# The norm's factor leaves the first half's input projection and enters behind it

## The chip, the cores and the metric

The kernel runs on one core of a Trainium2 chip. The metric is the device time of one execution in microseconds; of several runs the median counts. Engines are named as in the profile: PE is TensorE, DVE is VectorE, ACT is ScalarE, POOL is GpSimd, SP is SyncE, which issues all DMA transfers here.

## The reference

One decoder layer on x of 2048 positions by 1024 features, all in float32. Cut to what the change touches:

```python
h = rmsnorm(x, norm1_g)              # h = x * f * g, f = rsqrt(mean(x*x) + eps) for each position
proj = h @ w_in
p_q, p_k, p_v, p_g, p_a, c_b, c_c, c_h = split(proj)
q, k, v = p_q * 64**-0.5, p_k, p_v   # 4 heads, 64 wide for q and k, 128 for v
log_a = log_sigmoid(p_a @ w_gate_up + b_gate) / 16
o = gla_chunked(q, k, v, log_a)      # gated linear attention with a carried state
o = rmsnorm(o, gla_norm_g) * silu(p_g)
u = c_c * c_h
o_conv = c_b * causal_depthwise_conv(u, conv_w)   # three taps along positions
x = x + concat(o, o_conv) @ w_out
h2 = rmsnorm(x, norm2_g)
x = x + (silu(h2 @ w_ffn_gate) * (h2 @ w_ffn_up)) @ w_ffn_down
out = rmsnorm(x, norm_f_g)
```

The factor f is one number for each position, so it can be taken out of the projection: proj is f times (x * g) @ w_in. The attention is linear in v; its output is normalised by head, so a factor of q drops out but for the small eps, and k and v enter as a product.

## The kernel before, in words

Positions are handled in four blocks of 512 (`PB`), two to a half. A tile has 128 partitions and 512 columns; features lie on partitions, positions on columns. The halves go one after the other through the input projection (`in_proj`), then both through the output projection and the feed-forward part.

The input projection of a half has twelve units. A unit makes a block of two output row tiles by two position blocks from four weight quarters (A11, A12, A21, A22; 128 by 512 each) and the input operands. Units 2 to 11 (`unit`) use seven products of sums and differences instead of eight (S1 to S4 of weights on POOL, T1 to T4 of inputs on POOL); each product is four contraction steps. Unit 0 (`build_first`) and unit 1 (`plain_unit`) use eight plain products, since the differences of inputs are made meanwhile (`differences`). Units 0 to 3 give k, q and v, units 4 and 5 the swish gate (`silu`), units 6 to 11 the convolution: 6 and 9 give c_c, 7 and 10 c_h, 8 and 11 c_b.

Every float32 operand is split in two (`split`): ACT copies it to a rounded high part (L153), DVE subtracts that from it for the low part (L154). A step is then three matmuls: high by high, high by low, low by high (L366 to L368 in a unit; L297 to L299 in unit 0). The weight quarters are split so too (`weight_quarter`), into a pool of four buffers (`wqp`), so splits run at most four quarters ahead. Operands (`op`) have 28 buffers; the x rows of the norm share them.

In the beginning `first_loads` loads, in this order: x rows of block 0 (positions on partitions, for the squares), the weights of unit 0 and the input tiles `h` of block 0 (from `xt`, which is x with features on partitions), x rows of block 1, the input tiles of block 1. `row_squares` sums the squares on ACT, `rows_rstd` makes the factor (Ln and Exp on ACT, a Newton step on DVE), spreads it and transposes it on PE into a PSUM bank (`rb_ps`), and `scaled` (L490) multiplies an input tile by gain and factor in place. Then the tile is split and multiplied.

Work beside the units is written as generators in a list (`background`); `tick`, called after each product, runs one step of the first of them. In the first half these are, in turn, `gate_weights`, a pause, `row_stats` of blocks 2 and 3, `gate` (the forget gate: Abs, Exp, Ln on ACT, scans on DVE), `h1_ahead` (the second half's operands) and, from unit 6 on, `gla_half`. A scheduler sets each engine's final order from the program and its dependences; each engine then runs its instructions strictly in that order.

## Time and profile before

| | |
|---|---|
| median of 3 runs | 2110.91 us |
| lowest and highest | 2108.93 and 2113.38 us |
| profiled execution, span from first to last instruction | 2109.1 us |
| profiled execution, its own time | not listed apart from the span |
| PE, DVE, ACT, POOL busy | 2033.1, 1418.4, 1014.1, 972.4 us |
| mean granted clock of PE | 0.992 |
| HBM traffic | 219 GB/s over the span |

A row of the timeline gives the start in us from the span's start, the duration, engine, line, operation, output<-inputs, partitions x elements, and in brackets how long the engine stood idle before and what ended that. A row of waits gives the waiting instruction, what it waited for, the total, how often, and the longest. A row of a group gives its count, then busy time and the mean of one in ns, then the idle time before. A row of windows gives a stretch, its length, and the busy time of PE, weight loads, DVE, ACT and POOL (with counts), the granted clock, the DMA share and GB/s.

### The profile page before, as it was taken

What the parts mean: (1) busy time and instruction counts of PE and PEld (TensorE: products, weight loads), DVE (VectorE), ACT (ScalarE), POOL (GpSimd) and SP (SyncE); (2) the same over time, 40 slices, a digit from 0 to 9 for tenths busy, and PEclk for the clock granted to TensorE, in tenths of its full rate; (3) what the DMA queues carried; (4) which work ended last, traced back from release to release, by engine and by line L of the source; (5) the groups of instructions that cost most, each with busy time, mean ns of one, the idle gap of its engine ahead of it and who ended that gap; (6) DMA issues with size and microseconds to landing.
All of it is one profiled execution on the core that took longest, in us unless ns stands there. A gap on an engine that the chain in (4) does not pass through costs nothing.

```text
span 2109.1 us, 26874 instructions
## 1 busy us (share of the span) xinstructions
PE 2033.1 (96%) x9133; PEld 1648.9 (78%) x9133; DVE 1418.4 (67%) x1983; ACT 1014.1 (48%) x1997; POOL 972.4 (46%) x703
## 2 busy tenths in 40 slices
PE   5999999999999999999999999999999989999996
PEld 4778888877888878788888878787888868877775
DVE  7669786549753786788786665554766666665564
ACT  5555455656542356445545443333554554543344
POOL 3436322222102464564464348764645544436774
PEclk9999999999999999999999999999999999999998
DMA  7349485425586872656545687697454535587763
GB/s 277 126 158 318 139 329 164 148 83 164 201 284 235 325 249 100 241 198 221 217 172 220 243 327 272 235 338 296 158 207 179 206 134 190 183 344 281 269 269 110
DMA packets 189241, 464.43 MB, mean 220 GB/s; under 512 B 19824, under 2 KB 65072, under 8 KB 179504
## 3 DMA queue, kind: packets, MB, share of 16 engines
q1 hardware_dynamic: 189104, 462.72, 60.4%
q8 instruction: 72, 1.18, 0.2%
q14 instruction: 65, 0.53, 0.1%
HBM read 297.49 MB, written 165.15 MB: 219 GB/s over the span
## 4 chain that ended last, share of the span: by engine, by line
PE 70%; DVE 8%; DMA 7%; ACT 3%; issue 3%; POOL 2%; SPq 0%; DVEq 0%; ACTq 0%; POOLq 0%
PE mm L366 21%; PE mm L368 21%; PE mm L367 21%; DVE wq L154 2%; DMA op<-shT 1%; DVE so L154 1%; PE mm L794 1%; DVE h L490 1%; PE mm L795 1%; PE mm L797 1%; DVE op L154 1%; DMA sx<-y 1%; ACT wq L153 1%; PE o_ps L718 1%; DMA shT<-so 1%
## 5 line engine op out<-in xcount | busy, mean ns | idle before, releaser
L366 PE MATMUL mm<-op,wq 128*128 128x512 f32 x2499 | 981.3, 395 | 23.8 <-DVE c L390 7.8
L368 PE MATMUL mm<-op,wq 128*128 128x512 f32 x2499 | 966.1, 392 | 12.6 <-DVE wq L154 11.9
L367 PE MATMUL mm<-op,wq 128*128 128x512 f32 x2499 | 976.0, 391 | 0.0
L154 DVE TENSOR_TENSOR wq<-raw,wq 128x512 fp32r<-128x512 f32 (+2 forms) x626 | 527.3, 849 | 329.9 <-ACT wq L153 324.3
L153 ACT ACTIVATE wq<-raw 128x512 fp32r<-128x512 f32 (+2 forms) x626 | 363.6, 587 | 555.8 <-PE mm L368 402.4
L366 PEld LDWEIGHTS mm<-op,wq 128*128 128x128 f32 x2499 | 470.8, 188 | 137.6 <-ACT wq L153 12.3
L368 PEld LDWEIGHTS mm<-op,wq 128*128 128x128 f32 x2499 | 470.5, 188 | 123.5 <-DVE wq L154 24.8
L367 PEld LDWEIGHTS mm<-op,wq 128*128 128x128 f32 x2499 | 471.2, 189 | 96.7 <-issue 1.0
L351 POOL TENSOR_TENSOR raw<-s,raw 128x512 f32<-128x512 f32 (+2 forms) x97 | 127.5, 1314 | 422.2 <-DVE wq L154 402.0
L390 DVE TENSOR_TENSOR c<-mm,c 128x512 f32<-128x512 f32 x267 | 183.0, 686 | 95.7 <-PE mm L368 93.0
L349 POOL TENSOR_TENSOR s<-raw 128x512 f32<-128x512 f32 (+2 forms) x97 | 130.2, 1343 | 216.2 <-DMA raw<-in_wffn_dram 88.8
L356 POOL TENSOR_TENSOR raw<-raw 128x512 f32<-128x512 f32 (+2 forms) x97 | 126.7, 1306 | 135.3 <-DVE wq L154 128.1
L386 ACT ACTIVATE c<-mm 128x512 f32<-128x512 f32 x267 | 154.7, 585 | 38.0 <-PE mm L368 36.8
L776 POOL TENSOR_TENSOR ssx<-ssx,q 128x512 f32<-128x512 f32 x52 | 76.5, 1483 | 156.0 <-ACT q L775 155.8
L350 POOL TENSOR_TENSOR raw<-raw 128x512 f32<-128x512 f32 (+2 forms) x97 | 135.1, 1393 | 4.1
L965 POOL TENSOR_TENSOR y<-c,y 128x512 f32<-128x512 f32 x66 | 98.7, 1499 | 49.0 <-DVE c L390 46.6
L154 DVE TENSOR_TENSOR so<-t,so 128x512 fp32r<-128x512 f32 x100 | 91.2, 918 | 25.9 <-ACT so L153 25.4
L153 ACT ACTIVATE wq<-s 128x512 fp32r<-128x512 f32 (+2 forms) x97 | 56.9, 586 | 93.5 <-PE mm L368 83.3
L794 PE MATMUL mm<-op,wq 128*128 128x512 f32 x256 | 100.9, 395 | 0.0
L795 PE MATMUL mm<-op,wq 128*128 128x512 f32 x256 | 99.8, 390 | 0.0
L154 DVE TENSOR_TENSOR wq<-s,wq 128x512 fp32r<-128x512 f32 (+2 forms) x97 | 84.1, 867 | 15.6 <-ACT wq L153 15.0
L153 ACT ACTIVATE so<-t 128x512 fp32r<-128x512 f32 x100 | 62.5, 627 | 41.8 <-DMA sa_T<-so 16.1
(177 smaller groups left out, 1885.0 us busy)
## 6 DMA issues: line engine op xcount, KB each, us to landing
raw<-in_wffn_dram SPq DMA_DIRECT2D x44, 1024.0 KB, 5.7
sa_T<-so SPq DMA_DIRECT2D x88, 512.0 KB, 5.3
op<-sa_T SPq DMA_DIRECT2D x88, 512.0 KB, 9.2
sa_B<-so SPq DMA_DIRECT2D x69, 512.0 KB, 3.4
op<-sa_B SPq DMA_DIRECT2D x69, 512.0 KB, 9.0
raw<-in_win_dram SPq DMA_DIRECT2D x23, 1024.0 KB, 5.5
raw<-in_wdown_dram SPq DMA_DIRECT2D x24, 768.0 KB, 6.2
sx<-y SPq DMA_DIRECT2D x48, 256.0 KB, 3.2
```

The source lines that it names most:

```text
L153: last_hi[:] = [act.activation(hi, src, AF.Copy)]
L154: return dve.tensor_tensor(lo, src, hi.bitcast(F32), ALU.subtract)
L349: pool.tensor_tensor(s1, a21, a22, ALU.add)
L350: pool.tensor_tensor(a21, a11, a21, ALU.subtract)
L351: pool.tensor_tensor(a11, s1, a11, ALU.subtract)
L356: pool.tensor_tensor(a12, a12, a11, ALU.subtract)
L366: pe.matmul(o[:], wh, xh, start=first and k == 0, stop=False, skip_group_check=True)
L367: pe.matmul(o[:], wh, xl, start=False, stop=False, skip_group_check=True)
L368: return pe.matmul(o[:], wl, xh, start=False, stop=k == n - 1, skip_group_check=True)
L386: act.activation(t[:], o[:], AF.Copy)
L390: dve.tensor_tensor(t[:], o[:], t[:], ALU.add)
L794: pe.matmul(o[e, j][:], wh, m[:, 0, :], start=k == 0, stop=False)
```

## The change

The first half's unit 0 takes input times gain only. ACT's copy to the high part and DVE's subtraction carry the gain, and POOL multiplies the tile by it in place for the later differences. The x rows, their squares and the factor move behind: the rows are loaded after all input tiles and after unit 1's weights, and the squares are a background task (`first_stats`). The factor then enters in the forget gate's input, the swish gate and c_c (c_c by its square; c_h is not multiplied), the convolution's result (once more), the value's copy in the attention (by its square, with positions on partitions) and, as a scale, the normalisation of the attention's output. Twelve matmuls of ones by ones stand at the start. The second half is as it was.

```diff
...
@@ -270,25 +270,37 @@
             put("B22", k, b22)
             yield
 
-    def build_first(quad, w):
+    def build_first(h, raw):
 
 
         ops = {b: [] for _, b in PRODUCTS}
-        h, o = {}, {}
+        o, out, w = {}, [], {}
         quarters = ("A11", "A12"), ("A21", "A22")
-        los = []
+        order = []
+
+        def turn(n, i):
+            with ExitStack() as stack:
+                if order:
+                    stack.enter_context(tc.issue_after(order[-1].ins))
+                w[n] = weight_quarter(raw[:, i, :])
+            order.append(last_hi[0])
+
         for j in range(2):
             for r in range(2):
                 o[r, j] = bank()
             for k in range(KD):
-                with ExitStack() as stack:
-                    if len(los) > 1:
-                        stack.enter_context(tc.issue_after(los[-2].ins))
-                    h[k, j] = quad(k, j)
+                g = col(C_G1 + k)
+                if j == 0 and k in (0, 3, 4):
+                    turn(*{0: ("A11", 0), 3: ("A12", 1), 4: ("A22", 2)}[k])
                 x = opp.tile([P, 2, PB], F32R, name="op", tag="op")
-                los.append(split(h[k, j][:], x[:, 0, :], x[:, 1, :]))
-                if j == 0 and k >= PT:
-                    row_squares(1, k - PT)
+                with tc.issue_after(order[-1].ins):
+                    order.append(act.activation(x[:, 0, :], h[k, j][:], AF.Copy, scale=g))
+                if (k, j) == (0, 0):
+                    turn("A21", 3)
+                dve.scalar_tensor_tensor(
+                    x[:, 1, :], h[k, j][:], g, x[:, 0, :].bitcast(F32), ALU.mult, ALU.subtract
+                )
+                pool.tensor_scalar(h[k, j][:], h[k, j][:], g, 1.0, ALU.mult, ALU.mult)
...
-            if j == 0:
-                rbs[1] = rows_rstd(squares[1])
-
+            out += [(r, j, settled(o[r, j], True), False) for r in range(2)]
         def differences(wanted):
             for n, y, a, b in (
                 ("T1", (0, 0), (0, 1), (0, 0)), ("T2", (0, 0), (4, 1), (0, 0)),
...
@@ -446,9 +455,26 @@
         dve.tensor_tensor(ssq[:, :, 0], ssq[:, :, 0], ssq[:, :, 1], ALU.add)
         rbs[b] = rows_rstd(ssq)
 
-    def rows_rstd(ssq):
-
-        v, l, y0 = [mtiny.tile([P, PT], F32, name=n, tag=n) for n in ("msq", "rl", "ry")]
+    def first_stats():
+        yield from pause(1)
+        for b in range(2):
+            for t in range(PT):
+                row_squares(b, t)
+                if t % 2:
+                    yield
+        yield from pause(3)
+        for b in range(2):
+            f, f2 = [mtiny.tile([P, PT], F32, name=n, tag=f"{n}{b}", bufs=1) for n in ("f", "ff")]
+            factors[b] = tiny.tile([P, PB], F32, name="rb", tag="rb")
+            act.activation(factors[b][:], rows_rstd(squares[b], f)[:], AF.Copy)
+            dve.tensor_tensor(f2[:], f[:], f[:], ALU.mult)
+            positions[b] = f, f2
+            yield
+
+    def rows_rstd(ssq, v=None):
+
+        l, y0 = [mtiny.tile([P, PT], F32, name=n, tag=n) for n in ("rl", "ry")]
+        v = v or mtiny.tile([P, PT], F32, name="msq", tag="msq")
...
-    rbs, raws, first_weights, last_load, rows, squares = {}, {}, {}, [], {}, {}
+    rbs, raws, positions, rows, squares, factors, factors2 = {}, {}, {}, {}, {}, {}, {}
 
     def row_squares(b, t):
         act.activation(rows[b, t], rows[b, t], AF.Square, accum_out=squares[b][:, t, 0:1])
@@ -466,6 +492,14 @@
     def first_loads():
 
         raw = rawp.tile([P, 4, PB], F32, name="raw", tag="raw")
+        for j in range(2):
+            for k in range(KD):
+                if j == 0 and k % 4 == 0:
+                    for i in ((0, 3), (1, 2))[k // 4]:
+                        raw_loads.append(load(raw[:, i, :], win[0][:, i, :]))
+                h = raws[k, j] = bt("h") if len(raws) > 4 else tt("h")
+                load(h[:], xt[j, :, k, :])
+        second = raw_weights(win[1])
         for b in range(2):
             squares[b] = mtiny.tile([P, PT, 2], F32, name="ssq", tag="ssq")
             for t in range(PT):
@@ -473,18 +507,7 @@
...
-            for k in range(KD):
-                if b == 0 and k % 4 == 0:
-                    for i in ((0, 3), (1, 2))[k // 4]:
-                        raw_loads.append(load(raw[:, i, :], win[0][:, i, :]))
-                h = bt("h") if b else tt("h")
-                raws[b, k] = h
-                last_load[:] = [load(h[:], xt[b, :, k, :])]
-        for t in range(PT):
-            row_squares(0, t)
-        rbs[0] = rows_rstd(squares[0])
-        for n, i in (("A11", 0), ("A21", 3), ("A12", 1), ("A22", 2)):
-            first_weights[n] = weight_quarter(raw[:, i, :])
+        return raw, second
 
...
-    def build_h():
-
-
-        def quad(k, j):
-            return scaled(col(C_G1 + k), rbs[j], raws[j, k])
-
-        return build_first(quad, first_weights)
+    def factored(c, in_psum, f):
+
+        s = tt("n") if in_psum else c
+        (dve if in_psum else pool).tensor_tensor(s[:], c[:], f[:], ALU.mult)
+        return s
 
     def h1_ahead():
 
@@ -560,7 +581,12 @@
                         stop=n == "B22" and k == 3 and e == 1, skip_group_check=True,
                     )
         a_sb = bt("a_sb")
-        act.activation(a_sb[:], a[:], AF.Copy)
+        if half:
+            act.activation(a_sb[:], a[:], AF.Copy)
+        else:
+            for j in range(2):
+                r = slice(32 * j, 32 * j + 32)
+                dve.tensor_tensor(a_sb[r, :], a[r, :], factors[j][r, :], ALU.mult)
         yield
         for j in range(2):
             small = decays[2 * half + j] = [
...
+        def values(u):
+            f = factors2 if u in (6, 9) else factors
+            for r, j, c, p in next(units):
+                if half == 0 and u in (4, 5, 6, 9):
+                    c, p = factored(c, p, f[j]), False
+                yield r, j, c, p
+
         def units():
             for u in range(12):
-                with ExitStack() as stack:
-                    if half == 0 and u == 1:
-                        stack.enter_context(tc.issue_after(last_load[0].ins))
-                    if half or u > 1:
-                        us = unit(win[u], ops)
-                    else:
-                        us = plain_unit(win[u], ops) if u else first
+                if half or u > 1:
+                    us = unit(win[u], ops)
+                else:
+                    us = plain_unit(second, ops) if u else first
                 if half == 0 and u == 1:
                     del ops["B12"]
                     differences(("T4",))
@@ -611,16 +641,21 @@
         units = units()
         if half == 0:
             differences(("T1", "T2", "T3"))
-        for dst, i0 in ((s_kq, 0), (s_kq, 2), (s_v, 0), (s_v, 2)):
-            for r, j, c, p in next(units):
+        for u, (dst, i0) in enumerate(((s_kq, 0), (s_kq, 2), (s_v, 0), (s_v, 2))):
+            for r, j, c, p in values(u):
                 store(dst[2 * half + j][i0 + r][:], settled(c, p)[:])
         for i0 in (0, 2):
-            for r, j, c, p in next(units):
+            for r, j, c, p in values(4 + i0 // 2):
                 store(s_g[2 * half + j][i0 + r][:], silu(c, p)[:])
         background.append(gla_half(half))
+        if half == 0:
+            for j in range(2):
+                factors2[j] = tiny.tile([P, PB], F32, name=f"rr{j}", tag=f"ssx{j}", bufs=1)
+                act.activation(factors2[j][:], factors[j][:], AF.Square)
         for i0 in (0, 2):
-            cc = {(r, j): settled(c, p) for r, j, c, p in next(units)}
-            ch = {(r, j): c for r, j, c, _ in next(units)}
+            u = 6 + 3 * (i0 // 2)
+            cc = {(r, j): settled(c, p) for r, j, c, p in values(u)}
+            ch = {(r, j): c for r, j, c, _ in values(u + 1)}
...
@@ -635,9 +670,11 @@
                         dve.scalar_tensor_tensor(
                             y[:], s[:, n : n + PB], col(C_CW + 4 * n + i), y[:], ALU.mult, ALU.add
                         )
+                    if half == 0:
+                        pool.tensor_tensor(y[:], y[:], factors[j][:], ALU.mult)
                 if half == 0:
                     act.activation(halo[:, i, :], left, AF.Copy)
-            for r, j, c, _ in next(units):
+            for r, j, c, _ in values(u + 2):
                 y = cc[r, j]
                 dve.tensor_tensor(y[:], c[:], y[:], ALU.mult)
                 hi = tp.tile([P, PB], F32R, name="hi", tag="t")
@@ -702,7 +739,10 @@
         for h in range(HEADS):
             pe.transpose(v_ps[:, h, :], v[:, h, :], ident[:])
         act.activation(kt[:, 0:2, :], kt_ps[:], AF.Copy)
-        act.activation(v[:], v_ps[:], AF.Copy)
+        if b in positions:
+            act.activation(v[:], v_ps[:], AF.Copy, scale=positions[b][1][:, t : t + 1])
+        else:
+            act.activation(v[:], v_ps[:], AF.Copy)
         if b or t:
             em = decays[b][0]
             for h in range(HEADS):
@@ -739,9 +779,12 @@
         ssq, l, y0 = [mtiny.tile([P, HEADS], F32, name=n, tag=n) for n in ("hsq", "hl", "hy")]
         sq = mtiny.tile([P, P], F32, name="sq", tag="rep")
         for h in range(HEADS):
-            act.activation(sq[:], o[:, h, :], AF.Square, accum_out=ssq[:, h : h + 1])
+            f = positions[b][0][:, t : t + 1] if b in positions else 1.0
+            act.activation(sq[:], o[:, h, :], AF.Square, scale=f, accum_out=ssq[:, h : h + 1])
         dve.tensor_scalar(ssq[:], ssq[:], 1.0 / P, EPS, ALU.mult, ALU.add)
         rsqrt(ssq[:], ssq[:], l[:], y0[:])
+        if b in positions:
+            dve.tensor_scalar(ssq[:], ssq[:], f, None, ALU.mult)
         osb = bt("osb", (P, HEADS, P))
         rs = ssq[:].rearrange("p (h c) -> p h c", c=1).to_broadcast([P, HEADS, P])
         dve.tensor_tensor(osb[:], o[:], rs, ALU.mult)
@@ -1046,19 +1089,22 @@
             scale(j, rbs[j])
 
 
+    warm = bank("warm")
+    for _ in range(12):
+        pe.matmul(warm[:, 0:P], ones[:], ones[:], start=True, stop=True)
     act.preload_act_table_set("natural_log_exp_and_others")
-    first_loads()
+    raw, second = first_loads()
     for i in range(4):
         load(wgu_sb[16 * i : 16 * i + 16, :], wgu[0:16, :])
-    ops, first, differences = build_h()
+    ops, first, differences = build_first(raws, raw)
     hurry.append(True)
     background.extend(
         [
-            gate_weights(), pause(9), row_stats(2), row_stats(3), gate(0, ops), unhurried(),
+            gate_weights(), first_stats(), pause(2), row_stats(2), row_stats(3), gate(0, ops), unhurried(),
             h1_ahead(),
         ]
     )
-    in_proj(0, ops, first, differences)
+    in_proj(0, ops, first, second, differences)
     drain_background(lambda: len(background) < 2)
     ops = load_pairs(s_h1)
     background.append(gate(1, ops))
```

The places where the order of ACT changes, each before and then of the changed kernel. First, ACT from its first instruction after the table load; `xr` is an x row, `wq` a weight quarter's split, `op` an input operand's high part, `rl` and `ry` the root.

```order
L464 ACTIVATE xr,ssq<-xr 128x1024 x4
L153 ACTIVATE wq<-raw 128x512
L158 ACTIVATE rl<-msq 128x4
L153 ACTIVATE wq<-raw 128x512
L159 ACTIVATE ry<-rl 128x4
L153 ACTIVATE wq<-raw 128x512 x2
L153 ACTIVATE op<-h 128x512 x3
L464 ACTIVATE xr,ssq<-xr 128x1024
```

```order
L153 ACTIVATE wq<-raw 128x512
L297 ACTIVATE op<-h,sml 128x512
L153 ACTIVATE wq<-raw 128x512
L297 ACTIVATE op<-h,sml 128x512 x2
L153 ACTIVATE wq<-raw 128x512
L297 ACTIVATE op<-h,sml 128x512
L153 ACTIVATE wq<-raw 128x512
L297 ACTIVATE op<-h,sml 128x512 x12
```

The four squares and the root leave the place ahead of the first operands; weight quarters and the sixteen operands come first.

Second, ACT where unit 1's first two weight quarters are split (the last `wq` rows of each piece; `op<-h` are the differences' high parts, `wa_sb` the gate's weights, `xn` rows of block 2).

```order
L153 ACTIVATE op<-h 128x512 x2
L153 ACTIVATE wa_sb<-wa 128x4x16 x3
L153 ACTIVATE op<-h 128x512 x2
L444 ACTIVATE xn,ssq<-xn 128x512
L153 ACTIVATE op<-h 128x512
L444 ACTIVATE xn,ssq<-xn 128x512
L415 ACTIVATE c_807<-mm 128x512
L153 ACTIVATE op<-h 128x512
L153 ACTIVATE wq<-raw 128x512 x2
```

```order
L490 ACTIVATE xr,ssq<-xr 128x1024
L153 ACTIVATE op<-h 128x512
L424 ACTIVATE c_637<-mm 128x512
L490 ACTIVATE xr,ssq<-xr 128x1024
L424 ACTIVATE c_639<-mm 128x512
L490 ACTIVATE xr,ssq<-xr 128x1024
L158 ACTIVATE rl<-f 128x4
L153 ACTIVATE op<-h 128x512
L490 ACTIVATE xr,ssq<-xr 128x1024
L153 ACTIVATE wq<-raw 128x512
L153 ACTIVATE op<-h 128x512
L153 ACTIVATE wq<-raw 128x512
```

Squares of x rows of block 1, which stood among unit 0's operands, now stand here; the last of the eight is directly ahead of unit 1's first quarter.

Third, ACT in units 4 and 5, where Silu of the swish gate (L422, now L431) meets the forget gate's Exp and Ln (L590 and L592; now L608, L609, L616).

```order
L590 ACTIVATE em<-g_1489 128x4
L422 ACT_TABLE_LOAD
L422 ACTIVATE c_1437<-c_1437 128x512
L153 ACTIVATE hi<-t_1625 128x512
L422 ACTIVATE c_1505<-c_1505 128x512
L592 ACT_TABLE_LOAD
L592 ACTIVATE el<-g_1490 128x4
L153 ACTIVATE wq<-raw 128x512 x2
L422 ACT_TABLE_LOAD
L422 ACTIVATE c_1473<-c_1473 128x512
L153 ACTIVATE hi<-t_1625 128x512
L153 ACTIVATE wq<-raw 128x512
```

```order
L609 ACT_TABLE_LOAD
L609 ACTIVATE g_1521<-g_1521,ones 128x512
L431 ACT_TABLE_LOAD
L431 ACTIVATE c_1435<-c_1435 128x512
L616 ACT_TABLE_LOAD
L616 ACTIVATE em<-g_1487 128x4
L608 ACTIVATE g_1552<-g_1552 128x512
L153 ACTIVATE wq<-raw 128x512
L609 ACT_TABLE_LOAD
L609 ACTIVATE g_1552<-g_1552,ones 128x512
L431 ACT_TABLE_LOAD
L431 ACTIVATE c_1470<-c_1470 128x512
```

The two kinds, which need different tables, now alternate; up to the attention's own table load there are 14 loads in ACT's order where there were 4. Each Silu of a value that is not in PSUM now follows a multiply on POOL.

7 lines of the change are left out of this document (3 added, 4 removed).

## The prediction

> **What bounds the kernel now.** I read the page's share of busy time first, then TensorE's waits over the first 400 us, then the timeline of the start.
>
> ```profile
> PE 2033.1 (96%) x9133; PEld 1648.9 (78%) x9133; DVE 1418.4 (67%) x1983; ACT 1014.1 (48%) x1997; POOL 972.4 (46%) x703
> ```
>
> TensorE is busy for 96% of the span, so a microsecond counts only where TensorE stands still or runs slowly. The waits of TensorE, 0 to 400 us (total, times, longest):
>
> ```profile
> PE rb_ps L458 <- DVE rep L457: 14.3, 2, 14.1
> PE mm L368 <- DVE wq L154: 4.2, 2, 2.1
> PE mm L297 <- ACT op L153: 3.8, 2, 2.3
> ```
>
> The largest is at the very start, and these three, but for half of the second, fall in the first 66 us. The timeline (start, duration, engine, line, instruction) shows why:
>
> ```profile
> 1.24 1.84 SPq L145 DMA_DIRECT2D xr<-in_x_dram  x4
> ...
> 4.88 1.06 ACT L464 ACTIVATE xr<-xr 128x1024 f32<-128x1024 f32 x1 [2.80 <-DMA xr<-in_x_dram]
> ...
> 6.83 1.06 ACT L464 ACTIVATE xr<-xr 128x1024 f32<-128x1024 f32 x1 [0.80 <-DMA xr<-in_x_dram]
> ...
> 14.07 1.45 PE L458 MATMUL rb_ps<-ident,rep 128*128 128x128 f32 x4 [14.07 <-DVE rep L457]
> ...
> 17.16 1.13 ACT L153 ACTIVATE op<-h 128x512 fp32r<-128x512 f32 x2
> ...
> 17.83 1.22 PE L297 MATMUL mm<-op,wq 128*128 128x512 f32 x2 [2.30 <-ACT op L153]
> ...
> 19.85 0.63 PE L298 MATMUL mm<-op,wq 128*128 128x512 f32 x1
> ...
> 20.28 0.63 PE L299 MATMUL mm<-op,wq 128*128 128x512 f32 x1
> ...
> 23.79 0.39 PE L298 MATMUL mm<-op,wq 128*128 128x512 f32 x1
> ...
> 24.02 0.39 PE L299 MATMUL mm<-op,wq 128*128 128x512 f32 x1
> ```
>
> The first transfers are rows of x (1.24), only for the norm. Their squares (4.88 on), the root and the transposes (14.07) precede the first projection matmul at 17.83. Its matmuls follow each other in 0.43 us (19.85 to 20.28) until 23.79 and in 0.23 us after: 5.96 us at half the rate, a loss of 3 us. It comes back later:
>
> ```profile
> 65.16 0.79 PE L368 MATMUL mm<-op,wq 128*128 128x512 f32 x1 [2.06 <-DVE wq L154]
> ...
> 71.24 0.40 PE L367 MATMUL mm<-op,wq 128*128 128x512 f32 x1
> ```
>
> After short waits TensorE is slow for another 6.1 us (65.16 to 71.24). The landmark by which I compare the kernels is the third product of the third unit, where the seven-product units get under way. ScalarE copies the first two products out here:
>
> ```profile
> 81.54 0.58 ACT L386 ACTIVATE c<-mm 128x512 f32<-128x512 f32 x1
> ...
> 84.32 0.58 ACT L386 ACTIVATE c<-mm 128x512 f32<-128x512 f32 x1
> ```
>
> So that product starts at 84.3. A unit of eight products is 96 matmuls, 21.8 us at 0.227; two of them and two products more are 21.8 + 21.8 + 5.4 = 49 us. Some 35 us of the 84.3 are start, waits and slow clock: that is all the change can win. Later TensorE is the bound, and what the front wins is kept unless later stages lose it.
>
> **The change, part by part.** *First matmul.* No x row stands ahead now; two quarter-megabyte weights and then the first input tile do. In the rows above 512 KB arrived at 4.88 and the next at 6.83, so 768 KB arrives at about 5.8. Split to matmul took 0.67 us (17.16 to 17.83): 6.5 us instead of 17.83. The 12 warm-up matmuls have no row; the nearest are the transposes at 14.07, of that shape, 4 in 1.45 us. Twelve take 4.4 us (at most 12 x 0.43 = 5.2), from about 1.1, when their operand is set: they end before 6.5 and cost nothing. If they bring full rate, unit 0 ends at 6.5 + 21.8 = 28.3; if not, at 31.3.
>
> *Second unit.* ScalarE's order puts all eight row squares ahead of this unit's first split, and the x rows are now last in the queue. Ahead of and with the eighth row 10.5 MB are moved. The windows (busy us of each engine, clock, DMA share, GB/s) give the rate:
>
> ```profile
> 0.00:10.00 10.00, 0.00 (x0) 0.00 (x0) 2.10 (x7) 5.14 (x8) 1.11 (x7) 1.00 0.74 259
> 10.00:20.00 10.00, 3.52 (x9) 2.13 (x10) 7.19 (x18) 4.90 (x11) 0.00 (x0) 1.00 1.02 357
> 20.00:30.00 10.00, 10.00 (x39) 8.07 (x38) 8.15 (x18) 7.28 (x16) 0.00 (x0) 1.00 0.99 361
> ...
> 40.00:50.00 10.00, 8.61 (x36) 6.55 (x37) 10.00 (x12) 7.97 (x19) 8.49 (x6) 1.00 0.53 185
> 50.00:60.00 10.00, 10.00 (x46) 8.28 (x45) 9.97 (x11) 4.59 (x14) 7.46 (x6) 1.00 0.45 157
> 60.00:70.00 10.00, 6.84 (x19) 4.80 (x18) 9.93 (x14) 10.00 (x26) 5.33 (x4) 0.72 0.53 182
> ...
> 80.00:90.00 10.00, 10.00 (x46) 8.28 (x45) 2.86 (x5) 3.70 (x7) 1.29 (x1) 1.00 0.21 65
> ```
>
> 259, 357 and 361 GB/s over 10 us each are 9.8 MB by 30; the eighth row lands at about 32. Its square (1.06) and the split (0.6) put the unit's start at 34: 3 to 6 us after unit 0, a new wait. One long enough for the slow clock, as before 65.16, so 3 us more. TensorE is through two units and two products at 34 + 21.8 + 5.4 + 3 = 64 (61 without the clock).
>
> By the Trainium skill (TensorE: Matmul & The Clock Gate, Part 1) the gate opens after one busy window of about 3.4 us. The rows show 5.96 and 6.1; by the page the loss would be 1.7, not 3, and the time 1.3 us less.
>
> *SyncE.* The input tiles now take the buffers that the gate weights and the later x rows had free, so their loads wait in SyncE's queue for GpSimd's differences, and stores and the fourth unit's weights stand behind them. ScalarE splits the gate weights ahead of the second half of unit 1's weights:
>
> ```profile
> wa<-in_wa_dram SPq DMA_DIRECT2D x1, 128.0 KB, 4.6
> ```
>
> The seventh difference comes at about 7 + 16 x 1.4 + 7 x 1.58 = 40 (prices below), the landing 4.6 later: 45. TensorE needs those weights at 34 + 10.9 = 45, or 48 if slow. It just fits; each microsecond later is one lost, up to the 66 below, which VectorE sets anyhow.
>
> *VectorE and GpSimd up to the landmark.* Can they feed it?
>
> ```profile
> 1.40 0.41 POOL L80 TENSOR_SCALAR_AFFINE_SELECT mask<-mask 128x256 f32<-128x256 f32 x1
> ...
> 18.09 0.69 DVE L154 TENSOR_TENSOR op<-h,op 128x512 fp32r<-128x512 f32 x1
> ...
> 49.35 6.98 DVE L154 TENSOR_TENSOR op<-h,op 128x512 fp32r<-128x512 f32 x6
> L310 POOL TENSOR_TENSOR h<-h 128x512 f32<-128x512 f32 x16 | 24.9, 1579 | 38.5 <-DVE h L490 33.2 <-DVE op L154 5.3
> L490 DVE SCALAR_TENSOR_TENSOR h<-h,sml,rb_ps 128x512 f32<-128x512 f32 x32 | 23.4, 738 | 1.0 <-PE rb_ps L458 1.0
> ```
>
> The scaling by norm and gain (L490, one operand in PSUM) goes: 16 x 0.74 = 12 us of VectorE, since the gain is now inside the low-half subtraction. That subtraction reads two SBUF tensors; such a one took 0.69 alone (18.09) and 1.16 each while GpSimd ran (six in 6.98). In order, 63 VectorE instructions precede and include the low half of the third product's weights. In 40 to 70 us, with GpSimd busy, 37 took 29.9 us, 0.81 each: 51 us from about 5, plus some 6 us in which they wait for the x rows (27 to 33): 62. GpSimd gets 16 gain multiplies without a row here. The bounds are twice the 128x256 select, 0.8, and L310's 1.58; I take 1.4, near the two-operand ones. With 16 differences at 1.58 and three weight sums that is 22 + 25 + 4 = 52 us from 7: 59. The last differences go GpSimd, ScalarE, VectorE in turn ahead of that product's weights, which adds some 4: 66, the latest of the three, is my value; bounds 61 (TensorE alone) and 69. The gain at the landmark is 84.3 - 66 = **18.3 us** (15 to 23).
>
> *Moved work.* The factor's eight transposes stood in the idle front and now stand among the third and fourth unit's products:
>
> ```profile
> 32.09 0.47 PE L458 MATMUL rb_ps<-ident,rep 128*128 128x128 f32 x2 [0.21 <-DVE rep L457]
> ```
>
> 0.24 each, 1.9 us, and 1 us of waits for their operand: **+3** (2 to 4). The copies and squares of the factor on ScalarE, and the row statistics, find the slack that 80 to 90 shows (VectorE 2.86 of 10, ScalarE 3.70); four more full ScalarE instructions would be 2.4 us if it were gone.
>
> *Gate and Silu.* The gate comes a few ticks later and its exponentials now alternate with the Silus: 14 table loads instead of 4 up to the GLA's.
>
> ```profile
> 150.89 1.28 ACT L592 ACT_TABLE_LOAD   x1
> 152.18 0.21 ACT L592 ACTIVATE el<-g 128x4 f32<-128x4 f32 x1
> 152.30 1.13 ACT L153 ACTIVATE wq<-raw 128x512 fp32r<-128x512 f32 x2
> 153.45 1.28 ACT L422 ACT_TABLE_LOAD   x1
> 154.74 0.63 ACT L422 ACTIVATE c<-c 128x512 f32<-128x512 f32 x1
> 155.28 0.62 ACT L153 ACTIVATE hi<-t 128x512 fp32r<-128x512 f32 x1
> ```
>
> A load takes 1.29 (150.89 to 152.18), a four-element instruction 0.12, a full one 0.54. From the first to the last split of the sixth unit stand 38: 9 loads, 5 small, 24 full: 11.6 + 0.6 + 13 = 25 us. TensorE needs 84 x 0.227 = 19.1 us for the unit, and the four weight buffers let splits run three products (8.2 us) ahead. The fifth split comes about 2 us late. Waits for GpSimd's multiplies can add to it. The stage already loses time:
>
> ```profile
> 151.46 0.50 PE L368 MATMUL mm<-op,wq 128*128 128x512 f32 x1 [2.11 <-DVE wq L154]
> ```
>
> I take **+2** (-1 to +9).
>
> By the Trainium skill (ScalarE: Activation LUTs, What ACT_TABLE_LOAD costs) a switch costs 2.66 us with its drain; the rows show no drain, and the sum goes by 1.29. What a drain would do is a rival below.
>
> *Factors.* Twenty GpSimd multiplies at 1.4 to 1.58 (12 on values, 8 on the convolution) are 30 us spread over some 150, beside TensorE's work; they slow VectorE's two-operand instructions. **+1** (0 to 4). The scale on the value copy is free, the extra four-element multiply in each of eight tiles is a microsecond in all, off TensorE's path. If that cover fails, it is the second rival.
>
> Sum: -18.3 + 3 + 2 + 1 = **-12.3 us**: span 2109.1 to 2096.8. The median lies 1.8 us above the profiled span, so **2098.5**.
>
> **Rivals.** *The chains keep up.* The landmark is set by TensorE: at 61 with the x-row wait, at 28.3 + 21.8 + 5.4 = 55.5 without. Gain 23 to 29 less 2: **2084 to 2090**. For it: VectorE has 12 us less. Against: it read 10.00, 9.97 and 9.93 of 10 in 40 to 70, and GpSimd now starts at 7 instead of 33. Chance 0.13.
>
> *VectorE stays the bound.* If all 46 large instructions cost 1.16 and 17 small 0.3, with the 6 us of waiting, VectorE needs 5 + 59 + 6 = 70 and the landmark is 72: gain 12, less 6: **2105**. For it: the six in 6.98. Chance 0.16.
>
> *Slower: ScalarE's queue blocks in the Silu stage.* Six Silus now wait for a GpSimd multiply, and weight splits queue behind them. In GpSimd's queue the multiplies stand among weight sums that wait for VectorE:
>
> ```profile
> L351 POOL TENSOR_TENSOR raw<-s,raw 128x512 f32<-128x512 f32 x13 | 19.5, 1497 | 84.1 <-DVE wq L154 84.1
> ```
>
> 84.1 us over 13, 6.5 each. If four of the six meet such a wait, 26 us less the lead of 8.2 is 18, with the loads 20: 18.3 - 3 - 20 - 1 = -5.7, **2116.5**. It turns slower from a loss of 18.5 us there. Against: three multiplies have a product's time or more before their Silu. Chance 0.08.
>
> *A drain at each table switch*, as long as the load: 9 x 1.29 more, a stall of 14 instead of 2: **2110.5**, no change. Against: 150.89 starts where the Silu before it ends. It is the page's rule above. Chance 0.03.
>
> **How the numbers follow.** The forecast (2092 to 2104) has 0.58, the rivals 0.13, 0.16, 0.08, 0.03, and 0.02 is left for a shift of later waits that eats it. 0.2% (4.2 us) is about what a measurement of this kernel tells from no change. Faster: 0.58 + 0.13 + 0.12 of the second = 0.83. Same: 0.04 + 0.03 + 0.02 = 0.09. Slower: 0.08. The range 2086 to 2109 takes in the bounds (23 with no later loss; 15 less 4, 6 and 4), most of the first two rivals, and leaves out 0.18.
>
> **What would show it.** Right: first projection matmul at 6 to 8 us; TensorE idle between the first two units until the eighth square, near 33; the copy after the second product near 66; short waits for weights where table loads alternate. Wrong: a landmark after 75, waits of over 3 us on Silu-stage splits, or TensorE's waits grown after 300 us.

## The result and the profile after

| | before | after |
|---|---|---|
| median | 2110.86 us (2108.93 to 2113.38) | 2131.68 us (2126.77 to 2134.14) |
| ratio to before, 95% interval | | 1.0098, 1.0085 to 1.0111 |
| profiled span, clock | 2109.1 us | 2129.5 us, 0.986 |

The change makes the kernel 1% slower, some 21 us, where the prediction had 12 us of gain and a range of 2086 to 2109. (A ratio, here and below, is the one on record; it can stand up to 0.1% beside the quotient of the medians shown.) The page's busy shares of the changed kernel:

```profile
PE 2048.7 (96%) x9157; PEld 1657.4 (78%) x9157; DVE 1431.3 (67%) x1983; ACT 1032.2 (48%) x2008; POOL 1025.6 (48%) x739
```

TensorE is busy for 15.6 of the 20.4 us by which the span has grown: 4.6 are the warm-up matmuls below, and the granted clock is lower behind the waits. The timeline of TensorE at the start:

```profile
1.12 4.59 PE L1094 MATMUL warm<-ones 128*128 128x128 f32 x24 [1.12 <-DVE ones L77]
7.73 1.32 PE L309 MATMUL mm<-op,wq 128*128 128x512 f32 x2 [2.02 <-ACT op L297]
...
31.16 0.39 PE L311 MATMUL mm<-op,wq 128*128 128x512 f32 x1
...
35.79 0.80 PE L375 MATMUL mm<-op,wq 128*128 128x512 f32 x1 [4.24 <-ACT wq L153]
...
74.42 0.79 PE L375 MATMUL mm<-op,wq 128*128 128x512 f32 x1 [8.69 <-ACT c L395]
```

The first projection starts at 7.73 instead of 17.83, and unit 0 is over at 31.5. Then 4.24 us of waiting between the units, as forecast, and at 65.7 a stop of 8.69 us that was not: the third product of unit 2 waits until ScalarE has copied the first one out of PSUM. ScalarE's timeline there (the squares of the late rows `xn` at L453, the copies at L395):

```profile
66.89 0.62 ACT L453 ACTIVATE xn<-xn 128x512 f32<-128x512 f32 x1
...
68.02 0.62 ACT L453 ACTIVATE xn<-xn 128x512 f32<-128x512 f32 x1
...
73.79 0.58 ACT L395 ACTIVATE c<-mm 128x512 f32<-128x512 f32 x1
...
75.67 0.58 ACT L395 ACTIVATE c<-mm 128x512 f32<-128x512 f32 x1
```

The copies, at 81.54 and 84.32 before, come 7.8 and 8.7 us sooner: half of the 18.3 that the sum took. By 257 us everything is gone and more. ScalarE's timeline has the last copy of unit 9, before and after in one fence each:

```profile
240.29 0.60 ACT L386 ACTIVATE c<-mm 128x512 f32<-128x512 f32 x1 [2.04 <-PE mm L368]
```

```profile
256.73 0.60 ACT L395 ACTIVATE c<-mm 128x512 f32<-128x512 f32 x1 [2.08 <-PE mm L377]
```

That is 16.4 us late; from 417 us on it is 19 to 20, and that stays. So 25 us are lost between 76 and 257 us and 3 behind it. The chain that ended last shows the first place, unit 5 (start, duration, engine, line):

```profile
145.87 1.28 ACT L431
147.81 1.28 ACT L616
150.37 1.28 ACT L609
152.41 1.28 ACT L431
154.35 1.28 ACT L618
```

Each of these is a table load: the forget gate's Ln (L609) and its two small Exp (L616, L618) alternate with Silu (L431), and weight splits stand behind them. The waits of TensorE (total, times, longest), 100 to 200 us and then the largest of 200 to 400 us:

```profile
PE mm L377 <- DVE wq L154: 3.2, 2, 2.9
PE mm L375 <- ACT c L395: 1.9, 1, 1.9
PE mm L375 <- ACT wq L153: 1.8, 1, 1.8
...
PE mm L377 <- DVE wq L154: 6.4, 9, 1.7
```

Before, these waits were 3.0 us from 100 to 200, and none is listed from 200 to 400. The windows (busy us of each engine with its instructions, clock, DMA share, GB/s), before and then after, show how VectorE falls behind in the later units:

```profile
100.00:120.00 20.00, 20.00 (x92) 16.30 (x91) 6.55 (x13) 5.62 (x10) 4.18 (x4) 1.00 0.25 93
120.00:140.00 20.00, 20.00 (x76) 13.61 (x76) 12.76 (x29) 12.96 (x26) 1.30 (x1) 1.00 0.27 92
140.00:160.00 20.00, 17.58 (x74) 13.28 (x72) 20.00 (x27) 12.92 (x23) 13.00 (x8) 1.00 0.79 270
```

```profile
100.00:120.00 20.00, 20.00 (x91) 16.38 (x90) 9.04 (x16) 6.02 (x11) 5.16 (x4) 1.00 0.29 105
120.00:140.00 20.00, 20.00 (x77) 13.30 (x75) 9.74 (x15) 8.27 (x13) 2.60 (x2) 1.00 0.15 53
140.00:160.00 20.00, 16.05 (x57) 12.01 (x57) 17.75 (x26) 19.28 (x28) 9.94 (x7) 0.87 0.43 145
...
220.00:240.00 20.00, 15.85 (x64) 11.25 (x62) 20.00 (x23) 8.36 (x17) 13.76 (x8) 1.00 0.47 149
```

From 100 to 140 VectorE is busy for 18.8 of 40 us, no more than before (19.3), though TensorE is 8 to 12 us further on: its background work has not come along. Behind that it is busiest (20.00 of 20 from 160 to 180 and 220 to 240), when the gate's scans, the second half's h and the convolution all want it.

### The profile page after: what moved, and what is told of

Same layout as the page of the kernel before. It is cut to its first block, busy times and chain, and to the rows that moved or that the text cites. A ratio compares the mean times of both kernels' runs of the same rounds, so it can differ in the third digit from the quotient of the medians.

```text
span 2129.5 us, 27006 instructions
## 1 busy us (share of the span) xinstructions
PE 2048.7 (96%) x9157; PEld 1657.4 (78%) x9157; DVE 1431.3 (67%) x1983; ACT 1032.2 (48%) x2008; POOL 1025.6 (48%) x739
## 4 chain that ended last, share of the span: by engine, by line
PE 72%; DVE 10%; DMA 6%; ACT 5%; issue 3%; POOL 3%; SPq 0%; DVEq 0%; POOLq 0%; ACTq 0%
PE mm L375 21%; PE mm L377 21%; PE mm L376 21%; DVE wq L154 2%; PE mm L837 2%; PE mm L838 2%; PE mm L840 2%; DVE h L513 1%; DVE so L154 1%; DMA raw<-in_wffn_dram 1%; DVE op L154 1%; DMA raw<-in_wdown_dram 1%; DMA h<-in_xt_dram 1%; ACT wq L153 1%; PE a_ps L579 1%
## 5 line engine op out<-in xcount | busy, mean ns | idle before, releaser
L395 ACT ACTIVATE c<-mm 128x512 f32<-128x512 f32 x267 | 154.9, 585 | 33.6 <-PE mm L377 32.0
L153 ACT ACTIVATE wq<-s 128x512 fp32r<-128x512 f32 (+2 forms) x97 | 56.7, 585 | 92.3 <-PE mm L377 85.3
```

The costliest lines, as they stand in the source:

```text
L153: last_hi[:] = [act.activation(hi, src, AF.Copy)]
L395: act.activation(t[:], o[:], AF.Copy)
```

## The experiments

Each ran beside the kernel before on its own chip, but the groups of experiments were on different chips, so runs of different groups are compared by their ratios. "Copies" are the starts of the first two copies in unit 2 and of the last in unit 9, in the profiled execution (before 81.5, 84.3, 240.3; after 73.8, 75.7, 256.7).

| run | edit, to which kernel | median us | ratio, 95% interval | copies |
|---|---|---|---|---|
| e1 | after, no factor multiplies | 2130.06 | 1.0083 (1.0066 to 1.0100) | 73.2, 75.1, 252.8 |
| e2 | after, gate ahead of the late rows' statistics | 2109.68 | 0.9987 (0.9975 to 0.9999) | 65.1, 69.3, 233.9 |
| e3 | after, late rows and gate 7 steps later | 2141.43 | 1.0137 (1.0118 to 1.0155) | 74.0, 75.9, 265.8 |
| e4 | before, gate 4 steps later | 2135.25 | 1.0108 (1.0090 to 1.0126) | 81.0, 83.8, 261.4 |
| e5 | before, with the multiplies (by ones) | 2123.49 | 1.0045 (1.0029 to 1.0061) | 79.0, 81.8, 252.2 |
| e6 | e2 without multiplies | 2097.26 | 0.9921 (0.9904 to 0.9938) | 65.4, 69.5, 225.2 |
| e8 | after, no pauses ahead of the gate, gate first | 2118.02 | 1.0023 (1.0013 to 1.0032) | 71.6, 82.2, 243.0 |
| e9 | before, 4 steps' pause behind the gate | 2112.39 | 1.0004 (0.9992 to 1.0017) | 78.7, 81.5, 237.5 |
| e10 | after, copy for Silu everywhere | 2124.89 | 1.0060 (1.0037 to 1.0083) | 74.0, 75.9, 253.8 |
| e11 | e2, second half's h spread out | 2108.69 | 0.9990 (0.9979 to 1.0001) | 65.4, 69.6, 234.8 |
| e12 | e2, all multiplies on VectorE | 2107.33 | 0.9979 (0.9967 to 0.9992) | 63.3, 68.9, 232.1 |
| e13 | e1, copy for Silu everywhere | 2112.60 | 1.0002 (0.9990 to 1.0015) | 74.5, 76.4, 247.5 |
| e14 | e2, convolution's multiplies on VectorE | 2107.27 | 0.9974 (0.9962 to 0.9986) | 65.2, 69.4, 232.9 |
| e15 | e2, those of its input on VectorE | 2108.06 | 0.9979 (0.9967 to 0.9991) | 63.6, 69.6, 234.0 |
| e16 | e4, copy for Silu everywhere | 2118.81 | 1.0029 (1.0015 to 1.0042) | 82.4, 85.2, 250.6 |
| e17 | e1, copy for Silu in the first half's swish gate | 2120.93 | 1.0040 (1.0027 to 1.0052) | 74.7, 76.6, 245.2 |
| e18 | e4, the same copy | 2125.55 | 1.0059 (1.0043 to 1.0075) | 81.6, 84.3, 251.4 |
| e19 | after, gate at its late place, the statistics behind it | 2144.35 | 1.0141 (1.0123 to 1.0160) | 64.8, 69.0, 267.4 |

**Multiplies or place?** The first four runs ask whether the loss is in the factors' multiplies or in the order of the background work.

```
-  if half == 0 and u in (4, 5, 6, 9):                                  # e1
+  if half == 0 and u in ():                        (and no multiply of y)
-  first_stats(), pause(2), row_stats(2), row_stats(3), gate(0, ops),
+  first_stats(), pause(2), gate(0, ops), row_stats(2), row_stats(3),   # e2
+  first_stats(), pause(9), row_stats(2), row_stats(3), gate(0, ops),   # e3
-  gate_weights(), pause(9), row_stats(2), row_stats(3), gate(0, ops),
+  ... row_stats(3), pause(4), gate(0, ops),                            # e4
```

> The changed kernel without the twenty GpSimd and four VectorE multiplies by the factor on the swish gate, c_c and the convolution's result (this part of the computation is left out; the factor is still made and used in the forget gate and the attention). Theory M (the multiplies slow VectorE and GpSimd in units 5 to 9, 11 of the 29 us lost after the third unit): 2117 to 2122 us against 2131.7, and TensorE's waits on weight splits between 195 and 260 us fall from about 9 us to under 3. Rival G (the loss is all from the forget gate standing among the Silus): 2128 to 2132, and the waits of TensorE stay.

> The changed kernel with the forget gate ahead of the row statistics of blocks 2 and 3 in the background list. ACT's order then holds 2 table loads up to the attention's own instead of 14, and the rows' squares come later than the first product's copy of unit 2. Theory M plus G: the two ScalarE losses go (about 12 us at unit 2 with the slow clock after it, about 8 in units 4 and 5), the multiplies' 11 stay: 2109 to 2114. Rival G alone: all is given back, 2095 to 2101. Rival F (the front gains no more than the 8.6 us seen): 2122 to 2126.

> The changed kernel with the pause ahead of the row statistics of blocks 2 and 3 at 9 steps instead of 2, so both they and the forget gate come later. Theory Q (the third product of unit 2 waited 8.7 us because ScalarE's copy of the first product stood behind the squares of late-loaded rows): the wait goes and the copy after the second product starts at 63 to 68 us instead of 75.7; the total is 2119 to 2126 with the gate's clash kept or worse. Rival F (another thing sets that point): the copy stays at 73 or later and the total at 2129 or more.

> The kernel before with a pause of 4 steps between row statistics and the forget gate, nothing else. ACT's order then holds 13 table loads up to the attention's own where there were 4, as in the changed kernel. Theory G (the alternation of Silu and Exp or Ln costs by itself): 2117 to 2123 against 2110.9. Rival M alone: 2109 to 2113, the loads are hidden by the four weight buffers.

Taking the multiplies away gives almost nothing back (e1, in the range of rival G). Moving two items of a list gives 22 us back (e2): the copies of unit 2 come at 65.1 and 69.3, and no `xn` square stands ahead of them. ScalarE's timeline of e2:

```profile
65.09 0.59 ACT L395 ACTIVATE c<-mm 128x512 f32<-128x512 f32 x1
...
69.28 0.58 ACT L395 ACTIVATE c<-mm 128x512 f32<-128x512 f32 x1
```

e3 was meant to move the squares out of unit 2 by a longer pause; ScalarE still ran 16 of them between 44 and 80 us, so it tells nothing on that, though its numbers are those of rival F, and only makes the gate later. e4 is the cleanest: the kernel before, with nothing but its gate four steps later, loses 1.1%, as much as the whole change and more than theory G's 2117 to 2123. TensorE's timeline there:

```profile
166.01 0.79 PE L366 MATMUL mm<-op,wq 128*128 128x512 f32 x1 [12.51 <-ACT wq L153]
```

From 130 to 176 us ScalarE has 15 table loads in e4, 13 in the changed kernel and 3 in the kernel before. Not all of them are between Silu and the gate. Ahead of the first Silu the gate's Exp (L582) and Ln (L583) follow each other without a load; behind it each loads a table, also when no Silu stands between them. ScalarE's timeline of before, then of e4:

```profile
126.64 0.63 ACT L582 ACTIVATE g<-g 128x512 f32<-128x512 f32 x1
127.31 0.73 ACT L583 ACTIVATE g<-g,ones 128x512 f32<-128x512 f32 x1
```

```profile
158.05 1.28 ACT L582 ACT_TABLE_LOAD   x1
...
159.99 1.28 ACT L583 ACT_TABLE_LOAD   x1
```

**The price of the multiplies, and of lateness.** e5 and e6 price the multiplies where the gate is early, e8 puts the gate earlier still, e9 delays only what follows the gate.

```
+  (dve if in_psum else pool).tensor_tensor(s[:], c[:], f[:], ALU.mult) # e5, f = 1.0
+  pool.tensor_tensor(y[:], y[:], factors[j][:], ALU.mult)
-  yield from pause(3)                              # e8, in first_stats
+  first_stats(), gate(0, ops), row_stats(2), row_stats(3), unhurried(),
+  row_stats(3), gate(0, ops), pause(4), unhurried(),                   # e9
```

> The kernel before, with the change's 20 multiplies on GpSimd and 4 on VectorE put into it at the same places (swish gate, convolution's input and output), by a tile of ones; its four table loads and its early gate stay. Theory M, that the factors cost by GpSimd and VectorE sharing their time in the stages in which VectorE is full: 2119 to 2123, TensorE waiting on VectorE in units 6 to 8. Theory L, that the loss comes from the gate and what follows it being late, and the factors cost little by themselves: 2111 to 2114.

> The changed kernel with the gate ahead of the late rows' statistics (as in the run before that did this) and without the factors' multiplies in the swish gate and the convolution: the computation lacks these factors. The gate-first run gained some 20 us by 118 us and lost 12 of them in units 6 to 8. Theory M, that the multiplies take these 12: 2096 to 2101. Theory L, that VectorE's work is late there whoever multiplies: 2105 to 2109.

> The changed kernel with all the pauses of the background work ahead of the gate taken out (3 steps in the statistics of the first rows, 2 after them) and the gate ahead of the late rows' statistics: the gate's VectorE work starts some 5 steps sooner. Theory L, that the background's lateness is what units 6 to 8 pay for: 2098 to 2105, below the gate-first run's 2110. Theory M: 2108 to 2112, as the gate-first run.

> The kernel before, with four steps of pause after the gate, so that only what comes behind it (the second half's h and the scans' preparation) is later, and the gate and its four table loads stay where they were. Theory L in its general form, that any background work that comes later falls into stages in which VectorE is full: 2118 to 2124. Theory T, that the lateness matters only for the gate, whose Exp and Ln then alternate with Silu's table: 2110 to 2113.

The multiplies cost 11.7 us in the kernel before (e5) and 12.4 with the early gate (e6 against e2) by medians, 10 and 14 by ratios: theory M was right on e6, and e5 lies half a microsecond above its range. VectorE's groups from 140 to 240 us show how, e2 (with) and then e6 (without); count, total and mean ns:

```profile
L154 DVE TENSOR_TENSOR wq<-raw,wq 128x512 fp32r<-128x512 f32 x28 | 31.7, 1148 | 1.7 <-ACT wq L153 1.6
...
L513 DVE SCALAR_TENSOR_TENSOR h<-h,sml,rb_ps 128x512 f32<-128x512 f32 x12 | 8.8, 736 | 2.1 <-DMA h<-in_xt_dram 2.1
L670 DVE SCALAR_TENSOR_TENSOR c<-u,sml,c 128x512 f32<-128x512 f32 x6 | 7.6, 1260 | 0.0
```

```profile
L154 DVE TENSOR_TENSOR wq<-raw,wq 128x512 fp32r<-128x512 f32 x31 | 27.6, 896 | 9.3 <-ACT wq L153 9.2
L513 DVE SCALAR_TENSOR_TENSOR h<-h,sml,rb_ps 128x512 f32<-128x512 f32 x11 | 8.1, 740 | 3.1 <-DMA siT<-lo 1.9 <-DMA h<-in_xt_dram 1.1
L670 DVE SCALAR_TENSOR_TENSOR c<-u,sml,c 128x512 f32<-128x512 f32 x8 | 7.9, 1003 | 0.0
```

The weight's low-half subtraction takes 1148 ns instead of 896: 28 of them are 7.1 us of VectorE, and the convolution's taps (1260 against 1003) 1.5 more. Both read two SBUF operands. The one with an operand in PSUM (L513) does not change. Not every group of two SBUF operands grows, though: `lo<-t,hi` takes 995 ns with the multiplies and 1077 without.

e8 missed both ranges. Without the pause the factor's transposes reach TensorE before their operand is there, and everything behind them waits:

```profile
64.82 0.69 PE L483 MATMUL rb_ps<-ident,rep 128*128 128x128 f32 x2 [5.03 <-DVE rep L482]
```

The slow clock follows. The second copy of unit 2 falls back to 82.2, but this includes 32 matmuls of the gate itself (L578, 7.9 us), which stand in unit 3 in e2; by the last copy of unit 3 e8 is 12.5 us behind e2 (116.2 against 103.7). e9 shows no cost of four steps of delay behind the gate (its interval ends at 3.6 us), as theory T has it; it is the gate's own place that counts.

**Table alternation or VectorE's work?** A copy in place of Silu leaves ScalarE's function table alone: from 130 to 176 us e10, e17 and e18 have no table load. What a late gate costs in these runs is not alternation.

```
-  last_silu[:] = [act.activation(s[:], c[:], AF.Silu)]
+  last_silu[:] = [act.activation(s[:], c[:], AF.Copy)]         # e10, e13, e16
+  ... AF.Silu if half else AF.Copy     (first half's swish gate) # e17, e18
+  first_stats(), pause(12), gate(0, ops), row_stats(2), row_stats(3),  # e19
```

> The changed kernel with a plain copy in place of Silu in both halves' swish gate (it leaves Silu out), so that ScalarE's order holds no table load after the first while the gate keeps its late place. Theory A, that the late gate costs by its Exp and Ln alternating with Silu's table, which blocks ScalarE's queue: 2108 to 2117, and the waits on ScalarE between 120 and 165 us are gone. Theory B, that VectorE's work of the late gate collides with the full stages behind it: 2124 to 2131.

> The changed kernel without the factors' multiplies in the swish gate and the convolution and with a copy in place of Silu (it leaves both out), the gate at its late place. Alone, the multiplies gave 1.6 back (2130.1) and the table's alternation 6.8 (2124.9). Theory H, that each hides the other (TensorE waits for whichever is left): 2105 to 2113. Theory B, that the late gate's VectorE work costs by itself, whatever is around it: 2119 to 2124, about the sum of the two alone.

> The kernel before with its gate four steps later (which alone gave 2135.3) and a copy in place of Silu (left out), so that there is no table to alternate with. Theory A, alternation makes the 24 us: 2110 to 2115. Theory B, VectorE's late work does: 2126 to 2133.

e10 lies in theory B's range, but with the multiplies in. e13, in theory H's range, and e16, between its two, seemed to say that alternation is most of the loss. Their last copy of unit 9 contradicts it: still 7.2 and 10.3 us late. The copy had also removed Silu's table loads in the second half and the feed-forward, and 6 to 8 us of the gain came from there (e16 against e18, e13 against e17, by ratios). The next two leave those stages alone.

> As the run without multiplies and with a copy for Silu (2112.6), but the copy stands in the first half's swish gate alone; Silu stays in the second half and in the feed-forward, where that run also lost its table loads. In that run the 24th copy after a product (a landmark in unit 9) came 7.2 us later than in the kernel before. Theory B, the late gate costs by itself and the 2112.6 came from later stages: 2119 to 2123. Theory H, the multiplies and the alternation hid each other: 2111 to 2114.

> The kernel before with its gate four steps later and a copy for Silu in the first half's swish gate alone (the run with the copy everywhere: 2118.8, its 24th copy 10.3 us late, against 21.1 with Silu). Theory A, alternation alone makes the late gate's cost: 2111 to 2116. Theory B, about half is VectorE's late work: 2119 to 2124.

> The changed kernel with a pause of twelve steps instead of two ahead of the gate, and the late rows' statistics behind the gate: the gate keeps about its late place while the row statistics leave the place ahead of unit 2. Theory R, the statistics cost the front 10 us by standing in ScalarE's queue: copies after the first products of unit 2 near 65 and 69 (73.8 and 75.7 in the changed kernel). If that gain lasts: 2120 to 2124. If the late gate swallows it: 2128 to 2133.

e17 is where theory B put it. With the gate late and neither multiplies nor alternation the kernel is still 25 us (1.0040 against 0.9921) behind e6, which differs in the place of the gate against the statistics and in that copy. e18, 1.6 us above B's range, agrees: of e4's 1.08%, alternation is 0.49 (10 us) and the rest, 0.59 (12 us), is there without it. The copies say where: from unit 4's last copy to unit 5's, e4 loses 15.3 us on before and e18 5.5; from there to unit 9's the two lose alike, 13.6 and 12.8. Where the 12 may come from stands in e18's windows, against those of before shown above:

```profile
120.00:140.00 20.00, 20.00 (x85) 15.55 (x84) 3.62 (x6) 6.46 (x12) 1.42 (x2) 1.00 0.22 79
140.00:160.00 20.00, 19.80 (x77) 13.65 (x75) 19.21 (x33) 12.78 (x26) 5.72 (x5) 1.00 0.42 145
160.00:180.00 20.00, 17.43 (x70) 14.28 (x71) 20.00 (x28) 11.10 (x21) 10.60 (x8) 0.91 0.83 289
...
200.00:220.00 20.00, 15.03 (x63) 11.78 (x64) 19.41 (x22) 9.96 (x21) 10.16 (x7) 1.00 0.82 277
220.00:240.00 20.00, 16.80 (x70) 12.57 (x69) 20.00 (x27) 9.00 (x18) 8.40 (x5) 1.00 0.60 201
```

VectorE worked 12.76 us from 120 to 140 before and works 3.62 here; these 9 us are owed later, and it is full from 140 to 180 and again from 200 to 240 (13.56 of 20 in between). TensorE's own waits from 120 to 260 us name ScalarE's copies for 7.2 us and VectorE for 3.5. One of the former leads back to VectorE: a small Exp of the gate waits for its scan (L587) in ScalarE's queue, and the copy stands behind it at 161.94.

```profile
161.82 0.21 ACT L590 ACTIVATE em<-g 128x4 f32<-128x4 f32 x1 [5.06 <-DVE g L587]
```

That VectorE's late work makes all of the 12 us is argued from these rows; no edit tried it by itself.

e19 bears out theory R: without the row squares ahead of them the copies come at 64.8 and 69.0. The front is then 19.0 us ahead at the last copy of unit 3 (92.3, before 111.3), and 27.1 behind at that of unit 9. Its windows:

```profile
100.00:120.00 20.00, 20.00 (x85) 15.54 (x84) 4.14 (x6) 4.72 (x9) 1.29 (x1) 1.00 0.08 27
120.00:140.00 20.00, 18.23 (x70) 12.01 (x68) 17.95 (x25) 17.84 (x26) 8.74 (x7) 1.00 0.41 145
140.00:160.00 20.00, 11.12 (x34) 8.01 (x34) 8.38 (x21) 19.84 (x43) 2.56 (x2) 0.78 0.73 242
160.00:180.00 20.00, 16.09 (x57) 12.23 (x58) 11.08 (x24) 19.60 (x34) 7.94 (x6) 0.84 0.31 114
...
240.00:260.00 20.00, 13.84 (x46) 10.03 (x46) 20.00 (x22) 6.62 (x13) 14.97 (x9) 0.83 0.77 264
```

The first large loss, 18.6 us from unit 4's last copy to unit 5's, falls mainly from 140 to 160, where ScalarE is full and VectorE less than half busy: from 120 to 180 us ScalarE has 18 table loads and the 16 squares, now moved there. A later one, 15.7 us from unit 8's to unit 9's, falls where VectorE is full. So the front's gain did not only fail to last: moving the squares put their work into the stage in which ScalarE was full of the gate's. This run came out above both ranges, and it does not separate VectorE's share from ScalarE's.

**A version that beats both.** With the gate early, can the multiplies be made cheaper?

```
-  if pace[0] % 2 == 0 or hurry:                                        # e11
+  if hurry or pace[0] % 5 in (0, 2) and slow or pace[0] % 2 == 0 and not slow:
...
-  (dve if in_psum else pool).tensor_tensor(s[:], c[:], f[:], ALU.mult)
+  dve.tensor_tensor(s[:], c[:], f[:], ALU.mult)           # e12, and y on dve
+  (dve if in_psum or factors2 else pool)...      # e14, and y on dve; e15 without
```

> The gate-first version of the changed kernel with the second half's h prepared in 2 steps of every 5 ticks instead of every second tick, so that its VectorE and GpSimd work (28 steps from 122 to 205 us) stretches to about 226 us and less of it lies in units 6 to 8. If these units are slow because the sum of the engines' work is too dense there: 2101 to 2106. If one unit's own work (weight sums, multiplies, convolution) is what is late: 2108 to 2112, as the gate-first run's 2109.7.

> The gate-first version of the changed kernel with the factors' 20 GpSimd multiplies on VectorE instead. Theory G, that the multiplies cost by standing in GpSimd's queue (1.6 us each, GpSimd 17.5 of 20 us busy from 160 to 180) ahead of the weights' sums: 2098 to 2105. Theory V, that VectorE (19.9 of 20 us there) is the limit and takes 20 more instructions of 0.7 us: 2112 to 2120.

> The gate-first version with the factors' multiplies of the convolution's input and output on VectorE and those of the swish gate still on GpSimd. The version with all of them on VectorE measured 2107.3, and the copies of unit 5 came 2.5 us later in it than with the swish gate's on GpSimd. If that is kept to the end: 2103 to 2106; if it is lost again in units 6 to 8: 2107 to 2110.

> As the run beside it, but only the convolution's input is multiplied on VectorE (6 multiplies more there), its output on GpSimd. Theory G, GpSimd's queue ahead of the weights' sums is the limit: 2104 to 2108, between 2109.7 and the run beside it. Theory V, VectorE is: 2109 to 2113.

Spreading the second half's h does nothing measurable (e11 is in its second range). With the multiplies on VectorE itself (e12) the median is 2.4 us below e2's and lies between the two theories' ranges, but the intervals overlap. The weight subtraction is back near its mean without the multiplies (949 ns, below), while VectorE carries 20 instructions more.

```profile
L154 DVE TENSOR_TENSOR wq<-raw,wq 128x512 fp32r<-128x512 f32 x29 | 27.4, 949 | 3.2 <-ACT wq L153 3.2
```

e14 is in the range for a gain that is lost again, and e15 falls just above theory G's. The intervals of e2, e12, e14 and e15 overlap, so that the multiplies became cheaper is not shown. e14 computes all that the changed kernel does and is 0.26% (0.14 to 0.38) faster than before and 1.2% faster than the change as it was made.

## Why the prediction was wrong, by its own steps

The profiled span came out 20.4 us longer where the sum had 12.3 less. Of these 33 us, 10 are missing at the landmark; 23 were lost behind it, where the sum had allowed 6 and the runs show 29. The step that failed is thus the pricing of the later stages, above all of the gate's new place.

- **First matmul, second unit** (right). 7.73 against 6.5 forecast; unit 1 at 35.79 against 34, after a wait of 4.24, with the slow clock behind it. The warm-up matmuls cost nothing; behind them the full rate held from the start only in some executions (0.23 us a matmul from 8.5 us on in e2, 0.43 until 11.4 in the profile of the change).
- **The landmark** (its size missed). "66 ... 18.3" measured 75.67 and 8.7. The step placed VectorE's and GpSimd's work and left the row statistics to "the slack that 80 to 90 shows". They do not run in 80 to 90: they stood in ScalarE's queue ahead of the first product's copy. With them behind the gate the copy is at 69.28 (e2) and 68.96 (e19), at the upper bound of 69. A landmark after 75 was among the prediction's own signs of being wrong. The gain multiply on GpSimd, priced at 1.4, took 1.14 on the mean; no wait of TensorE up to the landmark is put down to it.
- **Gate and Silu, "+2"** (failed). The step priced the alternation of "a few ticks later" by ScalarE's busy time alone, against the splits' lead of 8.2 us. Taken out, the alternation was worth 9 us (e1 to e17) and 10 us (e4 to e18), the step's upper bound. And it left out what a late gate costs besides, which had no term in the sum and is 12 us in e18; that this is VectorE's late work is the reading of the windows, shown for one wait only.
- **Factors, "+1 (0 to 4)"** (failed in size, though not in the change itself). 12 us with an early gate (e5; e2 against e6); 2 to 3 in the change itself, within the noise, where TensorE waits for other things as well. That the term's range holds there is luck. The rows for an estimate were in the prediction: a two-operand subtraction at 0.69 alone and 1.16 beside GpSimd loses 0.4 of each microsecond, and 20 x 1.6 x 0.4 = 13 us if all of it is owed where VectorE is full. By the Trainium skill (SBUF — State Buffer, "SBUF: two separate sides") a VectorE instruction with two SBUF operands and a GpSimd instruction that reads SBUF use a shared pair of ports, which whichever starts first holds for its whole instruction, and the other waits. The weight subtractions of e2 and e6 agree, 1148 against 896 ns, and so do 736 against 740 with an operand in PSUM; `lo<-t,hi` does not.
- **"What the front wins is kept unless later stages lose it"** (the sentence on which the sum stood). Units 5 to 9 are not TensorE's once the gate is late: e19 turned 19 us of lead into 27 of loss, while e6, with the gate early, kept 15 of 19.
- **Moved work and the scale on the value copy.** The moved transposes cost no wait of TensorE (L484, 65.34 to 89.46 us). From 257 to 442 us, where the attention's tiles of the first half run, the changed kernel loses 3 us more (16.4 to 19.5 us late; e6 -15.1 to -12.1), where the sum had a microsecond off the path; e4, e5 and e18, made from the kernel before, lose nothing there. "The scale on the value copy is free" had no row and is wrong: with it the copy takes 685 ns, without it 592 (the groups below), and 32 squares of the attention's output take 365 against 273, 3.7 us of ScalarE in all. Whether this makes the 3 us was not tried.
- **The rivals.** The slower one named the stage and the mechanism (weight splits behind Silu and table loads) but gave it 0.08 and let it stop at 2116.5; the waits for GpSimd's multiplies that it counted on were not it. The drain rival falls: a load at 147.81 stands 0.02 us behind the Silu before it and is followed at 149.11 by its own instruction. The 2.66 us a switch, with its drain, of the Trainium skill (ScalarE: Activation LUTs, What ACT_TABLE_LOAD costs) show in no run here.

ScalarE's groups of the value copy in the changed kernel, with the scale (first half) and without (second half):

```profile
L743 ACT ACTIVATE vt<-v_ps,ff 128x512 f32<-128x512 f32 x8 | 5.5, 685 | 0.1
...
L745 ACT ACTIVATE vt<-v_ps 128x512 f32<-128x512 f32 x8 | 4.7, 592 | 1.5 <-PE v_ps L740 1.5
```

The loss, taken apart by ratios x 2111 us: from the change 3 us go with the multiplies (e1), 9 with the alternation (e17), 25 with the gate and the row statistics in e2's order (e6), which is 17 us below before. Of the 25, the third copy of unit 2 shows 10.8 already (81.33 in e17, 70.52 in e6), the row squares' part; the rest arises later, and that it is VectorE's late work is argued. Each has some 4 to 5 us of uncertainty, so that the 3 are not clear of noise, and they depend on order: with the gate early the multiplies are worth 12, and with the gate late the squares' part does not last (e19).
